# Row sums on VectorE in place of TensorE scores for the far cache rows of the sample attention

## The chip, the cores and the metric

The kernel runs on one core of a Trainium2 chip. The metric is the device time of one execution in microseconds (us). Engines are named as in the profile: PE is TensorE (with PEld, its weight loads), DVE is VectorE, ACT is ScalarE, POOL is GpSimd, SP is SyncE, which issues most DMAs here.

## The reference

One decoder layer is computed for a prompt of 2048 positions and for 8 sample batches of 8 new positions each. Each sample batch has its own cache of 2048 key rows and 2048 value rows of 8 heads by 64. The part that the change touches is the attention of the samples:

```python
DILATED_CONFIGS = ((128, 1), (512, 4), (2048, 16))
...
def _dilated_branch_sample(q, k_all, v_all, dil, n_strides):
    T = q.shape[1]
    E = q.shape[-1]
    w_buf = k_all.shape[1] - T
    idx = w_buf + jnp.arange(T)[:, None] - dil * jnp.arange(n_strides + 1)[None, :]
    valid = idx >= 0
    idx = jnp.maximum(idx, 0)
    kg = k_all[:, idx]
    vg = v_all[:, idx]
    s = jnp.einsum('bthe,btjhe->bthj', q, kg).astype(jnp.float32) * (E ** -0.5)
    s = jnp.where(valid[None, :, None, :], s, -jnp.inf)
    m = jnp.max(s, axis=-1, keepdims=True)
    p = jnp.exp(s - m)
    den = jnp.sum(p, axis=-1)
    o = jnp.einsum('bthj,btjhe->bthe', p, vg.astype(jnp.float32)) / den[..., None]
    lse = m[..., 0] + jnp.log(den)
    return o, lse
```

The three results are then mixed with weights proportional to their denominators. A cache row more than 512 positions back belongs to the configuration with distance 16 alone. New position t (0 to 7) reaches there the rows 16p + t and no others: such a row has exactly one query, and the rows 16p + 8 to 16p + 15 have none.

The rest is, for prompt and samples: RMS norm, one projection to 3584 columns (u, v, gate of mixer A; q, k, v, gate of mixer B), partial rotation of q and k, the spatial gate of mixer A, the three dilated attentions of the prompt, gates and norms, the product with w_out, the residual and a last norm.

## The kernel before

**Stages.** Up to about 95 us weights are loaded, scaled and split into two 16-bit parts (`load_weights`, whose VectorE steps are lines 202 to 220), and the tiles of x are scaled and split (`row_scale`, line 327, whose steps follow each other across POOL 334, DVE 335 and 336, PE 338 `ps_r`, DVE 340 `ss`, DVE 346 `dg`, PE 348 `ps_d`, ACT 350 `rb`). From there to about 390 us PE makes the q, k and v columns of 16 prompt tiles and one sample tile (products on line 265: 24 matmuls of 128x512 for a tile and a weight). From 390 to about 905 us runs the attention of the prompt and mixer A. From 905 us to the end come the gates, the merge of the three results and the products with w_out, again with line 265.

**The sample attention is filler.** `Sample` (line 469) is a generator. `Filler.pull` (line 94) is called for each product matmul and adds 216 times a rate to what is owed; each step of the generator pays `STEP1` = 250 (batches 0 to 4, beside the q, k, v products) or `STEP3` = 333 (batches 5 to 7, beside the last stage). So its instructions stand spread among the matmuls of line 265. What the generator hands out is then ordered by a scheduler on a simulated time line; every engine runs its list in order.

**One batch.** Cache keys come in five chunks of 2 rows by 128 partitions, 512 KB each (`load`, line 489, tile `kr`). Chunks g = 0 to 3 are the rows 16p + 2g and 16p + 2g + 1 for all 128 p, chunk 4 the other residues of the last 512 rows. For each chunk PE transposes the keys (line 594, eight 128x128 f32), ACT copies them out of PSUM (line 597, `kt`), PE multiplies them with `qbd`, the queries of two heads in a block-diagonal operand of 16 columns (line 498), and DVE adds the mask (line 506) into `sm`, which holds 11 slots of 64 scores for 128 partitions. `attend` (line 510) then takes the maximum (lines 515 to 521), subtracts it (527), exponentiates on ACT, sums (529, `ps_n` 534), and multiplies with the value rows (line 547: the values are the weights, 16 columns of `sm` move), whose result is scaled into `ott` (line 557). `vn` and `ktn` are the new positions' own values and keys. An f32 product of lines 498 and 547 is recorded as two matmuls, a transpose as one.

## Time and profile before

| | |
|---|---|
| median of three runs | 1214.53 us (1210.95 to 1216.84) |
| profiled execution | 1221.7 us, of which the span is 1219.6 us |
| mean granted TensorE clock | 0.965 of full speed |
| busy: PE, PEld | 1151.5 us (94%), 755.4 us (62%) |
| busy: DVE, ACT, POOL | 789.5 us (65%), 621.1 us (51%), 273.3 us (22%) |
| moved by DMA | 237.98 MB, mean 195 GB/s |

The span runs from the first to the last recorded instruction. Busy time of an engine is the sum over its instructions; overlapping matmuls are counted once. A share of the whole span is an average over stages that have different limits, so the rows further down are cut by stage.

### The profile page before, as it was taken

What the parts mean: (1) busy time and instruction counts of PE and PEld (TensorE: products, weight loads), DVE (VectorE), ACT (ScalarE), POOL (GpSimd) and SP (SyncE); (2) the same over time, 40 slices, a digit from 0 to 9 for tenths busy, and PEclk for the clock granted to TensorE, in tenths of its full rate; (3) what the DMA queues carried; (4) which work ended last, traced back from release to release, by engine and by line L of the source; (5) the groups of instructions that cost most, each with busy time, mean ns of one, the idle gap of its engine ahead of it and who ended that gap; (6) DMA issues with size and microseconds to landing.
All of it is one profiled execution on the core that took longest, in us unless ns stands there. A gap on an engine that the chain in (4) does not pass through costs nothing. (4 is left out here: it accounts for less than half of the span.)

```text
span 1219.6 us, 23145 instructions
## 1 busy us (share of the span) xinstructions
PE 1151.5 (94%) x8418; PEld 755.4 (62%) x8418; DVE 789.5 (65%) x2331; ACT 621.1 (51%) x1341; POOL 273.3 (22%) x294
## 2 busy tenths in 40 slices
PE   6689999999999998998999999799989999999997
PEld 2247777877767445665666676465636667676543
DVE  7853535444542677876887888867956565656773
ACT  5554434443442855765776767866754322322232
POOL 4422112112210032243334334432300000000110
PEclk9798999999997998998999999988999999999999
DMA  8667676767672997889979988987689868576652
GB/s 285 227 216 219 199 209 202 233 201 214 184 216 90 255 228 161 149 137 213 181 143 196 218 130 182 189 173 107 142 288 356 236 206 226 175 197 201 183 152 87
DMA packets 299026, 237.98 MB, mean 195 GB/s; under 512 B 189920, under 2 KB 240096, under 8 KB 298912
## 3 DMA queue, kind: packets, MB, share of 16 engines
q1 hardware_dynamic: 272848, 210.58, 68.8%
q10 hardware_dynamic: 26064, 25.92, 8.0%
q8 instruction: 66, 1.08, 0.4%
q14 instruction: 48, 0.39, 0.1%
HBM read 128.38 MB, written 63.24 MB: 157 GB/s over the span
## 5 line engine op out<-in xcount | busy, mean ns | idle before, releaser
L265 PEld LDWEIGHTS <-xh 128*128 128x128 f16 x2760 | 293.3, 113 | 222.8 <-issue 27.7
L934 DVE CUSTOM_DVE_ANT_0 sm<-ps_s,mk,qsi 128x256 f32<-128x256 f32 (+1 forms) x384 | 145.2, 420 | 64.1 <-PE ps_s L929 56.3
L942 ACT ACTIVATE sm<-sm,st 128x256 f32<-128x256 f32 (+1 forms) x384 | 145.7, 450 | 58.4 <-DVE st L937 53.2
L265 PE MATMUL ps_y<-wh_o,cT 128*128 128x512 f16 x528 | 169.0, 380 | 0.0
L964 POOL TENSOR_TENSOR p<-sm,p 128x256 f16<-128x256 f32 (+1 forms) x128 | 112.6, 886 | 233.0 <-ACT p L963 205.4
L498 PEld LDWEIGHTS ps_q<-qbd,kt 128*128 128x128 f32 x640 | 109.4, 191 | 22.9 <-issue 0.3
L153 POOL TENSOR_TENSOR sc<-sc,powers 128x1 f32<-128x1 f32 (+3 forms) x51 | 31.5, 618 | 410.0 <-DVE sc L1140 186.6
L547 PEld LDWEIGHTS ps_o<-sm,vr 128*128 128x128 f32 x640 | 108.2, 199 | 22.1 <-issue 1.3
L265 PEld LDWEIGHTS <-cT 128*128 128x128 f16 x800 | 82.0, 114 | 55.4
L265 PE MATMUL ps_y<-wl_o,cT 128*128 128x512 f16 x272 | 103.4, 380 | 0.0
L980 PE MATMUL ps_o<-vt,pT 128*128 128x65 f16 x600 | 79.5, 194 | 21.2 <-DMA pT<-p 21.2
L547 PE MATMUL ps_o<-sm,vr 128*128 128x16 f32 x640 | 92.6, 238 | 0.0
L498 PE MATMUL ps_q<-qbd,kt 128*128 128x16 f32 x640 | 91.9, 225 | 0.0
L265 PE MATMUL ps_p<-wh_k,xh 128*128 128x512 f16 x264 | 88.5, 386 | 1.6 <-ACT wh_k L217 1.5
L265 PE MATMUL ps_p<-wh_gb,xh 128*128 128x512 f16 x264 | 87.8, 388 | 1.2 <-DVE u L1069 1.0
L265 PE MATMUL ps_p<-wh_q,xh 128*128 128x512 f16 x240 | 83.8, 395 | 5.1 <-ACT xh L253 4.8
L265 PE MATMUL ps_p<-wh_v,xh 128*128 128x512 f16 x264 | 87.7, 378 | 0.3 <-DVE z L281 0.3
L265 PE MATMUL ps_p<-wh_va,xh 128*128 128x512 f16 x264 | 84.2, 385 | 1.9 <-ACT vt L383 1.3
L265 PE MATMUL ps_p<-wh_u,xh 128*128 128x512 f16 x264 | 83.9, 379 | 1.7 <-DVE z L281 1.7
L265 PE MATMUL ps_p<-wh_ga,xh 128*128 128x512 f16 x264 | 85.3, 385 | 0.0
L925 PE MATMUL ps_s<-k,q 128*128 128x256 f16 (+1 forms) x384 | 83.9, 258 | 0.4 <-DVE st L934 0.4
L929 PE MATMUL ps_s<-k,q 128*128 128x256 f16 (+1 forms) x384 | 82.8, 256 | 0.0
(308 smaller groups left out, 2544.1 us busy)
## 6 DMA issues: line engine op xcount, KB each, us to landing
vr<-cache_v SPq DMA_DIRECT2D x40, 512.0 KB
kr<-cache_k SPq DMA_DIRECT2D x40, 512.0 KB
xh<-xd SPq DMA_DIRECT2D x32, 512.0 KB
raw<-w_in SPq DMA_DIRECT2D x52, 256.0 KB
brd<-ob ACTq DMA_DIRECT2D x48, 264.0 KB
bt<-brd SPq DMA_DIRECT2D x16, 792.0 KB
vt<-vd ACTq DMA_DIRECT2D x48, 258.0 KB
vd<-vs SPq DMA_DIRECT2D x32, 258.0 KB
```

The costliest lines, as they stand in the source:

```text
L153: pool.tensor_tensor(out, src, powers[:out.shape[0], 0, 0:n], op=ALU.pow)
L265: ii = pe.matmul(out, l, r[:, k], start=(k == 0 and i == 0), stop=(k == 7 and i == len(ops) - 1))
L498: ii = pe.matmul(self.ps[:, c:c + 2 * T], k, ops[0][:, b, j], start=True, stop=True)
L547: ii = pe.matmul(po[:, j], v, sm[:, 2 * g + i, j * 2 * T:(j + 1) * 2 * T], start=False, stop=(g == NC - 1 and i == 2 and j == 3))
L925: ii = pe.matmul(out, q, kv[0], start=True, stop=False)
L929: keep(pe.matmul(out, q, kv[1], start=False, stop=True), "s")
L934: dve.tensor_tensor_reduce(sm[:, y].rearrange("p b k -> p (b k)")[:, 0:n], out, m, qsi[:, 3:4], -3e38, op0=ALU.add, op1=ALU.max, accum_out ...
L942: act.activation(sv, sv, AF.Exp, bias=self.st[:, 4 + u:5 + u], scale=1.0)
L964: (pool, dve)[x in DVELO].tensor_tensor(lo, sv, hi, op=ALU.subtract)
L980: keep(pe.matmul(po[:, u, 0:E + 1], hi, vv[:, vi, j, 0:E + 1], start=(b == 0), stop=False), "o")
```

## The change

The sample scores are split by the distance of the cache row. Rows below 1536 (`FAR` = 96 partitions of 16 rows, of which residues 0 to 7 are loaded) go to chunks g = 0 to 3; the last 512 rows, now as four rows to a partition, go to chunks 4 and 5. The order of the chunks in a batch is 0, 1, 4, 2, 3, 5.

- **Far chunk (32 in all).** Keys come as 96 partitions, 384 KB. A second DMA of 384 KB fills a tile `qb` with the two queries 2g and 2g + 1 of the batch, repeated on 96 partitions, read from a copy of the rotated queries in memory (`qsd`, a new DMA). DVE multiplies keys by queries in place (96x1024 elements) and reduces over the 64 elements of each head to 16 numbers a partition, straight into one slot of `sm`. There are no transposes, no copy, no score product and no mask. In `sm` the partitions 96 to 127 of that slot are set to a large negative number once a batch.
- **Near chunk (16 in all).** As before: eight transposes, two copies, eight score products (12 with the new rows in chunk 5), mask add.
- **Values.** All value products stay on PE. For a far row the weights are 96 rows high and only the two columns of `sm` that belong to the row's query and two heads move, instead of 16. The matmul count of a batch goes from 44 to 52 products, 32 of them of two columns.
- **Sizes.** `sm` has 6 slots in place of 11, so the maximum, subtract, exponential and sum run over 384 elements instead of 704. `dg` and `rb` of `row_scale` go from two buffers to one, `kt` in the last stage from four to three; there `qbd` holds three batches instead of eight.
- **Pace.** `STEP1` is 310, `STEP3` 480; a far chunk has four steps, a near chunk eight and its score steps. A batch has 116 steps in place of 139.

Over all eight batches the order lists of the two kernels hold: transposes 320 and 128, score products 352 and 160, value products 352 and 416 (256 of them far), copies on ACT 80 and 32, far multiplies and far reduces on DVE 0 and 32 each, cache loads 80 and 96 (the bytes are the same), `qb` loads 0 and 32.

The core of the diff:

```diff
-STEP1 = 250.0
-STEP3 = 333.0
-NK = 11
+STEP1 = 310.0
+STEP3 = 480.0
+NK = 6
+FAR = 96
...
-        dg = ph1.tile([P, P], F32, name="dg", tag="dg")
+        dg = ph1.tile([P, P], F32, name="dg", tag="dg", bufs=1)
...
-        rb = ph1.tile([P, P], F32, name="rb", tag="rb")
+        rb = ph1.tile([P, P], F32, name="rb", tag="rb", bufs=1)
...
+                if i == 0:
+                    sp.dma_start(qsd, qk)
...
-    NC = 5
+    NC = 6
+    FSTEP = 2
+    KORD = (0, 1, 4, 2, 3, 5)
...
         if g < 4:
-            return c[b].rearrange("(p r) c -> p (r c)", r=16)[:, 2 * g * W:(2 * g + 2) * W]
-        first = c[b, PAST - 4 * P + 8:PAST - 4 * P + 9, 0:1]
-        return bass.AP(tensor=c.tensor, offset=first.offset, ap=[[16 * W, 32], [2 * W, 4], [1, 2 * W]])
+            return c[b, 0:FAR * 16].rearrange("(p r) c -> p (r c)", r=16)[:, 2 * g * W:(2 * g + 2) * W]
+        return c[b, FAR * 16:].rearrange("(p r) c -> p (r c)", r=4)[:, 2 * (g - 4) * W:(2 * g - 6) * W]
...
+            if key == "kr" and g < 4:
+                q = self.qbs[u] = self.samk.tile([P, 2, W], F32, name="qb", tag="qb", bufs=2)
+                sp.dma_start(q[0:FAR].rearrange("p n c -> p (n c)"),
+                             qsd[b * T + 2 * g:b * T + 2 * g + 2].rearrange("t c -> (t c)")[None, :]
+                             .to_broadcast([FAR, 2 * W]))
...
+        def far(self, g, kr, qb, sm):
+
+            k = kr[0:FAR]
+            dve.tensor_tensor(k, k, qb[0:FAR], op=ALU.mult)
+            yield
+            o = sm[0:FAR, 0].rearrange("p (h t) -> p t h", t=T)[:, 2 * g:2 * g + 2]
+            dve.tensor_reduce(o, k.rearrange("p n (h e) -> p n h e", e=E), axis=AX.X, op=ALU.add)
+            yield
...
+                        c = slice(j * 2 * T, (j + 1) * 2 * T)
+                        if g < 4:
+                            t = slice(2 * g + i, None, T)
+                            ii = pe.matmul(po[:, j, t], vr[0:FAR, i, j * P:(j + 1) * P], sm[0:FAR, 0, c][:, t],
+                                           start=False, stop=False)
+                        else:
+                            v = (vr[:, i] if i < 2 else self.vn)[:, j * P:(j + 1) * P]
+                            ii = pe.matmul(po[:, j], v, sm[:, 2 * g - 7 + i, c],
+                                           start=False, stop=(g == NC - 1 and i == 2 and j == 3))
...
                     if g == 0:
                         sms[b] = self.sam.tile([P, NK, G], F32, name="sm", tag="sm", bufs=3)
+                        dve.memset(sms[b][FAR:, 0], NEG)
...
+                    if far:
+                        next(fw)
+                        for _ in range(FSTEP):
+                            yield self.step
+                    elif b is not None:
                         ps = psT.tile([P, 2, 2 * P], F32, name="ps_k", tag="T")
```

How the change moves instructions is shown at three places. Line numbers of the changed kernel are higher by 2 to 36 (265 is 267 there, 220 is 222, 212 is 214, 547 is 571 for far rows and 575 for near ones, 534 is 556).

**PE among the products of k**, in the stage from 95 to 370 us. `ps_p` is the product of x (`xh`) and a weight's high or low part (`wh_k`, `wl_k`), `ps_q` a score product. Before:

```order
L265 MATMUL ps_p<-wl_k,xh 128x512
L498 MATMUL ps_q<-qbd,kt 128x16
L265 LDWEIGHTS xh
L265 MATMUL ps_p<-wh_k,xh 128x512
L265 LDWEIGHTS xh
L265 MATMUL ps_p<-wh_k,xh 128x512
L498 MATMUL ps_q<-qbd,kt 128x16
```

After, among the products of the same weight:

```order
L267 MATMUL ps_p<-wl_k,xh 128x512
L571 MATMUL ps_o<-sm,vr 128x2
L267 LDWEIGHTS xh
L267 MATMUL ps_p<-wh_k,xh 128x512
L571 MATMUL ps_o<-sm,vr 128x2
```

Between two matmuls of line 265 there is still one instruction of the sample attention, but here a value product of two columns and not a score product of 16; the far chunks have none of the transposes and score products any more.

**DVE while the third weight (`wl_v`) is prepared**, between 51 and 68 us of the trace of before. `ws_v` and `wg_v` are its scales, `ropa` and `ropb` the rotation of q and k. Before:

```order
L210 TENSOR_SCALAR ws_v<-ws_v 128x1
L220 SCALAR_TENSOR_TENSOR wl_k<-raw,wg_k,wh_k 128x512
L211 RECIPROCAL ws_v<-ws_v 128x1
L213 TENSOR_SCALAR ws_v<-ws_v 128x1
L314 TENSOR_SCALAR qsi<-ws_v 128x1
L322 TENSOR_TENSOR ropa<-qk,ropc 128x128
L323 TENSOR_TENSOR ropb<-qk,rops 128x128
L212 TENSOR_SCALAR wg_v<-ng,ws_v 128x8
```

After:

```order
L529 TENSOR_REDUCE sm<-kr 96x2x8
L212 TENSOR_SCALAR ws_v<-ws_v 128x1
L342 TENSOR_SCALAR ss<-ps_r 128x1
L326 TENSOR_TENSOR qk<-ropa,ropb 128x8x8
L327 TENSOR_TENSOR qk<-ropa,ropb 128x8x8
L283 TENSOR_TENSOR z<-ps_p,z 64x512
L213 RECIPROCAL ws_v<-ws_v 128x1
L215 TENSOR_SCALAR ws_v<-ws_v 128x1
L316 TENSOR_SCALAR qsi<-ws_v 128x1
L526 TENSOR_TENSOR kr<-kr,qb 96x1024
L348 TENSOR_SCALAR dg<-ident,ss 128x128
L214 TENSOR_SCALAR wg_v<-ng,ws_v 128x8
```

The far multiply (line 526) and reduce (line 529) of the first chunks now stand in DVE's list between the steps of the scale `wg_v` (line 212 before, 214 after). In all, four far multiplies and three far reduces stand ahead of the last `wl_v` step.

**PE at the end of the q, k and v products**, where the last of batches 0 to 4 is finished; `ps_o` is a value product. Before:

```order
L265 LDWEIGHTS xh
L265 MATMUL ps_p<-wh_q,xh 128x512
L547 MATMUL ps_o<-sm,vr 128x16 x16
L547 MATMUL ps_o<-sm,vn 128x16 x4
L265 LDWEIGHTS xh
L265 MATMUL ps_p<-wh_q,xh 128x512
```

After:

```order
L267 LDWEIGHTS xh
L267 MATMUL ps_p<-wl_q,xh 128x512
L571 MATMUL ps_o<-sm,vr 128x2 x8
L267 LDWEIGHTS xh
L267 MATMUL ps_p<-wh_q,xh 128x512
L267 LDWEIGHTS xh
L267 MATMUL ps_p<-wh_q,xh 128x512
L575 MATMUL ps_o<-sm,vr 128x16
```

Ahead of these rows both lists have a run of 24 value products (16 columns wide before, two after). The second run, 20 products long before, is eight long after, with the remaining ones spread among the products that follow.

## Rows read from the trace of the kernel before

**Rows 1.** Stages: us; busy of PE, PEld, DVE, ACT, POOL; PEclk; DMA share; GB/s.

```profile
95.00:370.00 275.00, 275.00 (x1923) 209.55 (x1922) 124.78 (x271) 115.93 (x194) 48.66 (x45) 0.99 0.69 209
905.00:930.00 25.00, 22.80 (x127) 13.20 (x125) 19.51 (x46) 13.11 (x25) 1.40 (x2) 0.93 1.06 384
930.00:1206.00 276.00, 276.00 (x1658) 174.14 (x1657) 170.83 (x346) 82.88 (x182) 19.21 (x31) 0.99 0.69 199
```

**Rows 2.** PE's timeline: start us, us, engine, line, operation.

```profile
200.67 0.27 PE L594 MATMUL ps_k<-ident,kr 128*128 128x128 f32 x1
200.78 0.38 PE L265 MATMUL ps_p<-wh_v,xh 128*128 128x512 f16 x1
...
206.38 0.29 PE L498 MATMUL ps_q<-qbd,kt 128*128 128x16 f32 x2
206.52 0.38 PE L265 MATMUL ps_p<-wh_q,xh 128*128 128x512 f16 x1
...
207.11 0.28 PE L338 MATMUL ps_r<-ones,sq 128*128 128x1 f32 x2
207.25 0.59 PE L265 MATMUL ps_p<-wh_q,xh 128*128 128x512 f16 x2
```

**Rows 3.** PE's timeline where the q products end; columns as in group 2.

```profile
368.89 5.91 PE L547 MATMUL ps_o<-sm,vr 128*128 128x16 f32 x44
374.64 0.59 PE L265 MATMUL ps_p<-wh_q,xh 128*128 128x512 f16 x1
...
378.43 6.85 PE L547 MATMUL ps_o<-sm,vr 128*128 128x16 f32 x32
...
386.82 0.59 PE L265 MATMUL ps_p<-wh_q,xh 128*128 128x512 f16 x1
```

**Rows 4.** That stretch in steps of 5 us; columns as in group 1.

```profile
370.00:375.00 5.00, 5.00 (x37) 4.74 (x37) 0.00 (x0) 0.00 (x0) 0.00 (x0) 0.78 0.75 230
375.00:380.00 5.00, 5.00 (x18) 2.96 (x16) 1.61 (x5) 2.02 (x4) 0.00 (x0) 0.50 0.14 51
...
390.00:395.00 5.00, 5.00 (x26) 2.44 (x25) 1.50 (x9) 2.59 (x8) 0.00 (x0) 1.00 0.00 0
```

**Rows 5.** DVE by line: ns of one (least/median/most), first to last start.

```profile
L1293 DVE TENSOR_TENSOR bt<-bt x16: 672/682/694, 912.5 to 1181.2; 128x512 f32<-128x512 f32 x16
L1292 DVE TENSOR_TENSOR bt<-bt,f x16: 1749/1758/1760, 908.9 to 1178.9; 128x1536 f32<-128x1536 f32 x16
L515 DVE TENSOR_REDUCE mx<-sm x8: 1349/1362/1370, 127.8 to 1093.3; 128x64 f32<-128x704 f32 x8
L520 DVE TENSOR_REDUCE mx<-ps_x x8: 271/282/283, 134.6 to 1104.8; 64x1 f32<-64x128 f32 x8
L527 DVE TENSOR_TENSOR sm<-sm,ps_b x8: 880/887/889, 142.5 to 1109.4; 128x704 f32<-128x704 f32 x8
```

**Rows 6.** DVE's timeline while `wl_v` is prepared; columns as in group 2.

```profile
51.90 0.15 DVE L207 TENSOR_SCALAR ws_v<-ps_w 128x1 f32<-128x1 f32 x1
...
67.52 0.74 DVE L220 SCALAR_TENSOR_TENSOR wl_v<-raw,wg_v,wh_v 128x512 f16<-128x512 f32 x1
```

**Rows 7.** Two stretches around it; columns as in group 1.

```profile
65.00:70.00 5.00, 5.00 (x26) 2.30 (x25) 5.00 (x10) 2.81 (x5) 2.81 (x3) 1.00 0.69 195
...
70.00:95.00 25.00, 20.61 (x106) 11.52 (x105) 9.07 (x19) 11.85 (x22) 5.87 (x6) 0.96 0.73 224
```

**Rows 8.** What PE waited for, 85 to 370 us: total us, times, longest.

```profile
PE ps_d L348 <- DVE dg L346: 2.8, 1, 2.8
PE ps_k L594 <- ACT kt L597: 1.3, 1, 1.3
```

**Rows 9.** DVE, columns as in group 5; POOL's busy us, mean ns, idle before.

```profile
L336 DVE TENSOR_TENSOR sq<-sq x17: 221/292/1307, 8.0 to 325.3; 128x128 f32<-128x128 f32 x16, 128x64 f32<-128x64 f32 x1
...
L251 POOL TENSOR_TENSOR xt<-xt,rb 128x512 f32<-128x512 f32 x32 | 42.0, 1333 | 37.1 <-ACT rb L350 33.5 <-issue 3.6
```

**Rows 10.** SP's issues of the keys; columns as in group 5.

```profile
L489 SPq DMA_DIRECT2D kr<-cache_k x40: 328/399/4966, 46.0 to 1039.7; - x40
```

More of the change, by code (lines that the diff above doesn't have):

```diff
@@ L148, in kernel_body @@
     vsd = dram.tile([64, W], F32, name="vsd")
+    qsd = dram.tile([64, W], F32, name="qsd")
     hd = dram.tile([S + 64, W], F32, name="hd")
@@ L477, in __init__ @@
             self.sam, self.samk, self.step = sam, samk, step
-            self.mask = const(samk, "smask", [P, 10 + DB, T], a["c_smask"])
+            self.b0 = NB1 if sam is samk else 0
+            self.kts = 3 if sam is samk else 4
+            self.mask = const(samk, "smask", [P, 4 + DB, T], a["c_smask"])
             self.ps = pso.tile([P, W], F32, name="ps_q", bufs=1)
             self.po = pso.tile([P, 4, 2 * T], F32, name="ps_o", bufs=1)
-            self.raws = {"kr": {}, "vr": {}}
+            self.raws, self.qbs = {"kr": {}, "vr": {}}, {}
         def load(self, c, key, u):
@@ L488, in load @@
             r = self.raws[key][u] = pool_.tile([P, 2, W], F32, name=key, tag=key, bufs=3)
-            sp.dma_start(r.rearrange("p n c -> p (n c)"), cache_rows(c, *u))
+            b, g = u
+            n = FAR if g < 4 else P
+            sp.dma_start(r[0:n].rearrange("p n c -> p (n c)"), cache_rows(c, b, g))
+            if key == "kr" and g < 4:
[3 more added lines that the diff above has]
+                             .to_broadcast([FAR, 2 * W]))
         def scores(self, b, g, kts, sm):
-            o = (g // 2 % 2) * 4 + (g % 2) * 2
-            for i in range(2 if g < NC - 1 else 3):
+            x = g - 4
+            o = 4 * x
+            for i in range(2 + x):
                 for j in range(4):
@@ L537, in attend @@
             zero = ops[1][:, 0, DB * T:]
-            keep(pe.matmul(po.rearrange("p j c -> p (j c)"), self.raws["vr"][(b, 0)][:, 0, 0:P], zero,
+            keep(pe.matmul(po.rearrange("p j c -> p (j c)"), self.raws["vr"][(b, 0)][0:FAR, 0, 0:P], zero[0:FAR],
                            start=True, stop=False), "v")
@@ L545, in attend @@
                     for j in range(4):
-                        v = (vr[:, i] if i < 2 else self.vn)[:, j * P:(j + 1) * P]
-                        ii = pe.matmul(po[:, j], v, sm[:, 2 * g + i, j * 2 * T:(j + 1) * 2 * T],
-                                       start=False, stop=(g == NC - 1 and i == 2 and j == 3))
+                        c = slice(j * 2 * T, (j + 1) * 2 * T)
[7 more added lines that the diff above has]
+                                           start=False, stop=(g == NC - 1 and i == 2 and j == 3))
                         keep(ii, "v")
@@ L574, in batches @@
             bs = list(bs)
-            chunks = [(b, g) for b in bs for g in range(NC)]
+            chunks = [(b, g) for b in bs for g in KORD]
             nxt = iter(chunks)
@@ L587, in batches @@
                 kts = []
+                far = b is not None and g < 4
+                if far:
+                    fw = self.far(g, kr, self.qbs.pop((b, g)), sms[b])
                 for x in range(2):
-                    if b is not None:
+                    if far:
+                        next(fw)
+                        for _ in range(FSTEP):
+                            yield self.step
+                    elif b is not None:
                         ps = psT.tile([P, 2, 2 * P], F32, name="ps_k", tag="T")
@@ L595, in batches @@
                                 yield self.step
-                        kt = self.samk.tile([P, 2, 2 * P], F32, name="kt", tag="ktt", bufs=4)
+                        kt = self.samk.tile([P, 2, 2 * P], F32, name="kt", tag="ktt", bufs=self.kts)
                         act.activation(kt, ps, AF.Copy)
@@ L608, in batches @@
                         yield from self.stage(work)
-                if b is not None:
+                if b is not None and not far:
                     late.append((b, g, kts, sms[b]))
@@ L1388, in _constants @@
     t = np.arange(T)
-    p, i = np.arange(P), np.arange(10)[:, None]
-    key = np.where(i < 8, 16 * p + i, PAST - 4 * P + 16 * (p // 4) + 2 * (p % 4) + i).ravel()
+    p, i = np.arange(P), np.arange(4)[:, None]
+    key = (PAST - 4 * P + 4 * p + i).ravel()
     own = np.where(p // T == np.arange(DB)[:, None], PAST + p % T, 10 * PAST).ravel()
@@ L1394, in _constants @@
     n = sum(((dist >= 0) & (dist <= P * d) & (dist % d == 0)).astype(int) for d in (1, 4, 16))
-    m = np.where(n > 0, 8.0 * np.log(np.maximum(n, 1)), NEG).reshape(10 + DB, P, T).transpose(1, 0, 2)
+    m = np.where(n > 0, 8.0 * np.log(np.maximum(n, 1)), NEG).reshape(4 + DB, P, T).transpose(1, 0, 2)
     out["c_smask"] = np.ascontiguousarray(m.astype(f))
```

17 lines of the change are left out of this document (7 added, 10 removed).

## The prediction

> **What bounds the kernel now.** I read the busy time by stage first, since the averages over the span mix stages. From 95 to 370 us, where the q, k and v products run with five of the eight sample batches between them, PE is busy for 275.00 of 275.00 us, while DVE is busy for 124.78, POOL for 48.66, and the DMA share is 0.69 [rows 1]. From 930 to 1206 us, with the other three batches, PE is again busy throughout (276.00 of 276.00) and DVE for 170.83 [rows 1]. The waits of PE say the same: between 85 and 370 us there are two, 2.8 and 1.3 us [rows 8], and between 930 and 1206 us none. So in these two stages, half of the span, one us taken from PE's list is one us of time, as long as what takes its place elsewhere is not late. The sample attention is filler there: each of its PE instructions pushes the products of line 265 back by what it costs. The change has to be summed on PE, and DVE has to be tested for being late.
>
> **What an instruction costs PE.** Recorded durations overlap, so I read distances between starts, with a sample instruction between two products. A transpose moves the next product by 200.78 − 200.67 = 0.11 us, a score product (two records) by 206.52 − 206.38 = 0.14 us, and a two-record product of one column by 207.25 − 207.11 = 0.14 us [rows 2]. The last row matters: 1 column costs what 16 cost, so a two-column value product should cost 0.14 us too. Narrower value products are therefore no gain, and no loss either.
>
> **PE, the main sum.** Removed: 192 transposes × 0.11 = 21.1 us and 192 score products × 0.14 = 26.9 us. Added: 64 value products × 0.14 = 9.0 us. Net −39.0 us, of which five eighths (24) fall into the first stage and 15 into the last. If a removed score product had cost as much as a product in an unbroken run (below, 0.26 us) the gain would be larger; much of what is removed stands alone between two products, so I keep 0.14 and let this term run from −45 to −35.
>
> **The clock at the end of the q products.** There the last of the five batches is finished by two unbroken runs of value products: 22 of them from 368.89 to 374.64 (0.26 us each) and 20 from 378.43 to 386.82 (0.42 each) [rows 3]. The granted clock is 0.78 of full in 370 to 375, then 0.50, the 1.2 GHz level, and back at 1.00, the 2.4 GHz level, from 390 us [rows 4]. Nine products between the runs took 378.43 − 374.64 = 3.8 us, 0.42 each. Against 0.21 for a product and 0.14 to 0.2 for a value product, the stretch loses some 9 to 12 us. Changed, the first run is still there with 24 products, the second has eight, and the rest stands between products. Before, the clock rose within 3 us of mostly products after the second run; with the second run shortened, it should come back some 10 us sooner, or not if the spread value products keep it low. I take −4 us, from −8 to +2.
>
> **The start.** The scales of the third weight begin at 51.90 us, and its last low part is written from 67.52 to 68.26 us [rows 6]; products of that weight wait for it. DVE is full there, 5.00 of 5.00 us [rows 7]. The changed list puts four far multiplies and three far reduces ahead of that last low part, none of which has anything to hide under on DVE. Prices: a two-input operation on SBUF takes 682 ns for 512 elements and 1758 for 1536 [rows 5], 1.05 ns an element, so a multiply of 1024 takes 682 + 512 × 1.05 = 1.22 us. A reduce of 704 elements takes 1.362 us, 1.93 ns an element, and one of 128 takes 0.282 us [rows 5]; that gives 0.28 + 896 × 1.05 = 1.22 us as the low end (a step from one element to the next at the multiply's pace) and 1024 × 1.93 = 1.98 as the high end. The reduce of 704 reads with a stride and the far one reads contiguously, as the one of 128 does, so I take 1.3. Then 4 × 1.22 + 3 × 1.3 = 8.8 us come ahead of the third weight. PE is idle for 25 − 20.6 = 4.4 us in 70 to 95 us anyway [rows 7], part of which gives way to this delay: +5 us, from 0 to +12.
>
> **DVE in the two full stages.** 32 × (1.22 + 1.3) = 81 us are added. Per batch the maximum and the sum go from 1.36 to some 0.75 us, the subtract from 0.887 to some 0.5 [rows 5], and mask adds shrink, about 2 us, 16 in all. Net +65 us, 40 of it in the first stage. DVE then has 165 of some 250 us there, 66%, and 170.8 + 24 = 195 of 262 in the last stage, 74%. At the dearest prices (1.98 for the reduce, and 2.27 for a multiply that is 1.05 us longer) the 20 pairs of the first stage take 85 us: 125 + 85 − 10 = 200 of 250, still not the bound. DVE works in order, though, and behind each far multiply stand `ss` and `dg` of `row_scale`, the rotation, and the copies out of the products. A multiply whose keys or `qb` are late holds them all, and PE then waits at `ps_d` or at a product. The existing waits of that kind are 4.1 us together [rows 8]. I allow +1 us in the first and +2 us in the last stage, from 0 to +8.
>
> **What is taken at nothing.** Keys and values are the same bytes; 32 `qb` loads of 384 KB add 12.6 MB to 238. In the first stage 20 of them make 7.9 MB beside 209 GB/s × 275 us = 57 MB, which raises the share of 0.69 by some 0.1 [rows 1]. Only from 905 to 930 us are the engines of the DMA full (share 1.06, 384 GB/s [rows 1]); two to four loads fall there at about 1 us each: +2 us, 0 to +4. SP issues 49 more transfers at 0.40 us each [rows 10], 20 us in all; they lie beside PE's work as long as the loads come some chunks ahead of their use, and would cost those 20 us at most if each delayed a chunk that PE waits for. The 48 copies that ACT loses are off the path (115.93 of 275 us busy [rows 1]), and a single buffer for `dg` and `rb` costs nothing while a tile's `row_scale` is over before the next begins. The pace costs nothing either: 116 steps × 310 / (216 × 0.9) = 185 product matmuls a batch against 139 × 250 / 194.4 = 179 in the first stage, and with 480, 333 and a rate of 0.8 322 against 268 in the last, 967 in all of some 976 that there are; if the last batch came too late for them, its rest would run as an unbroken stretch, a few us.
>
> **Sum.** −39 − 4 + 5 + 1 + 2 + 2 = −33 us. For the profiled execution that is 1221.7 − 33 = 1189 us; it lies 7.2 us above the median of the three runs, 1214.53, against which the change will be timed, so 1214.5 − 33 = **1182 us**.
>
> **The rivals.**
>
> *DVE late on PE's path (slower).* If each far multiply stalls PE, by its transfers or by POOL, the gain goes at 33 / 32 = 1.0 us a multiply beyond what I have allowed. At 2 us each, 64 us, the time is 1214.5 − 33 + 64 = 1245. For it: `L336`, two inputs on DVE, takes 292 ns as a rule and 1307 at most, and the 32 POOL multiplications of line 251 are 1333 ns long [rows 9]; a far multiply is four times as long as most of DVE's steps there, and `row_scale` passes DVE, POOL and PE in turn. Against it: PE has 4.1 us of waits in the first stage now, with DVE idle for 275 − 125 = 150 us, and not one in the last stage, where DVE has 62% of the time filled. The Trainium skill ("SBUF — State Buffer", "Who interferes with whom") says that a DVE instruction with two SBUF inputs contends with a GpSimd instruction that reads SBUF. By that rule each of the far multiplies that meets line 251 is longer, and the spread of `L336` from 292 to 1307 ns agrees; but 20 × 1.0 us would leave DVE at 187 of 250 us, so it alone does not decide for this rival.
>
> *The two-column products are not cheap (no change).* If each of the 256 far value products costs the 0.26 us that one costs in an unbroken run [rows 3], since 24 to 32 of them come in a row with their own weights, 256 × 0.12 = 31 us come back: 1182 + 31 = 1213. For it: that run. Against it: the 0.14 us of a one-column product between products [rows 2], and that much of that run was slowed by the falling clock.
>
> *The start costs all of its delay and the clock does not come back earlier.* +12 and +2 in place of +5 and −4: 1182 + 13 = 1195. At the other end the delay is hidden, the clock is back early and PE's gain is 45: 1182 − 5 − 4 − 6 = 1167. Both are in the range.
>
> **How the numbers follow.** The forecast with its own spread, 1165 to 1203, gets 0.78, including both ends of the start; the no-change rival 0.08; DVE late 0.09, of which some third stays under its break-even; something unforeseen 0.05, on both sides. The forecast's own terms add up to −17 and +22 from 1182. The range 1165 to 1206 leaves about 0.2 out, mostly above. A measurement here tells from no change what is over 0.5%, 6 us: faster is below 1208.5. Faster 0.83, same 0.08, slower 0.09.
>
> **What would show it.** Right: no waits of PE in the two full stages, both shorter, by some 20 us and some 12; products 0.21 us apart with a two-column product at 0.14 between; far multiply and reduce near 1.2 and 1.3 us; DVE near two thirds busy in the first stage; the granted clock below 1.00 for less than 20 us at the end of the q products; first products of the third weight some 5 us later. Wrong: waits of PE for `dg`, for copies behind a far multiply or for a far reduce that sum to tens of us; two-column products 0.26 us apart; a stretch of sample work alone after the last product.

## The result and the profile after

The changed kernel takes 1224.6 us (median of 4 runs, 1220.99 to 1231.97) beside 1212.74 us of the kernel before on the same chip: a ratio of 1.0102, with a 95% interval from 1.0066 to 1.0138. It is **slower by 1.0%, some 12 us**, where 33 us less was forecast. Times and ratios, here and below, are of executions in the faster of the two states that this program shows. The profiled execution has a span of 1224.9 us at a mean granted clock of 0.954 (1219.6 us and 0.965 before).

The stages after, with the columns of [rows 1]:

```profile
95.00:370.00 275.00, 254.85 (x1581) 174.39 (x1579) 144.48 (x292) 92.05 (x148) 51.70 (x47) 0.95 0.76 218
905.00:930.00 25.00, 20.93 (x85) 8.99 (x84) 20.30 (x43) 10.21 (x19) 0.71 (x1) 0.86 1.06 278
930.00:1206.00 276.00, 269.63 (x1514) 159.97 (x1513) 185.69 (x366) 73.09 (x166) 19.33 (x31) 0.96 0.87 226
```

PE, which was busy in every microsecond of the two long stretches [rows 1], now idles for 20 us of the first and 6 us of the last, and its granted clock is 0.95 and 0.96 there, against 0.99. DVE is far from full (144 of 275 us in the first stretch). The DMA share rises to 0.76 and 0.87.

What PE waited for from 85 to 370 us, to set beside [rows 8] (total us, times, longest):

```profile
PE ps_d L350 <- DVE dg L348: 15.4, 5, 5.7
...
PE ps_p L267 <- ACT qk L373: 2.0, 1, 2.0
```

And what DVE waited for in the whole span, first line of the view:

```profile
DVE kr L526 <- DMA kr<-cache_k: 52.7, 20, 6.2
```

So PE waits for `dg`, and DVE, which makes `dg`, waits at 20 of the 32 far multiplies for their keys. The scene that repeats, on DVE's own timeline (start us, us; in brackets the idle time ahead and what ended it):

```profile
142.35 1.22 DVE L526 TENSOR_TENSOR kr<-kr,qb 96x1024 f32<-96x1024 f32 x1 [2.17 <-DMA kr<-cache_k]
143.50 0.28 DVE L348 TENSOR_SCALAR dg<-ident,ss 128x128 f32<-128x128 f32 x1
143.69 1.21 DVE L529 TENSOR_REDUCE sm<-kr 96x16 f32<-96x1024 f32 x1
...
152.25 1.22 DVE L526 TENSOR_TENSOR kr<-kr,qb 96x1024 f32<-96x1024 f32 x1 [4.42 <-DMA kr<-cache_k]
```

on SP's:

```profile
135.59 0.42 SPq L500 DMA_DIRECT2D kr<-cache_k  x1
...
144.93 0.33 SPq L500 DMA_DIRECT2D kr<-cache_k  x1
145.35 0.38 SPq L500 DMA_DIRECT2D vr<-cache_v  x1
153.50 0.31 SPq L503 DMA_DIRECT2D qb<-qsd  x1
154.11 0.35 SPq L231 DMA_DIRECT2D xt<-xT  x1
```

on PE's and on ACT's:

```profile
143.82 0.80 PE L350 MATMUL ps_d<-dg,ones 128*128 128x128 f32 x2 [1.59 <-DVE dg L348]
```

```profile
159.86 0.63 ACT L334 ACTIVATE sq<-xt 128x512 f32<-128x512 f32 x1 [9.88 <-DMA xt<-xT]
```

The load at 135.59 is used at 142.35, the next, at 144.93 (right after the reduce that began at 143.69 has ended), at 152.25: 7 us from issue to use, each time with DVE standing. `dg` at 143.50 stands behind the multiply and PE behind `dg`. After the load of values at 145.35 SP issues nothing until 153.50: the load of `qb` there needs the buffer that the multiply of 152.25 to 153.47 has just given back. A tile of x stands behind it, and ACT waits 9.88 us for it.

Where the time of the stages went (start of the first and of the last product, for two weights, before and then after):

```profile
L265 PE MATMUL ps_p<-wh_v,xh x264: 376/379/390, 66.9 to 413.0; 128*128 128x512 f16 x132
L265 PE MATMUL ps_p<-wh_q,xh x240: 376/378/634, 37.7 to 392.0; 128*128 128x512 f16 x120
```

```profile
L267 PE MATMUL ps_p<-wh_v,xh x264: 376/379/635, 66.9 to 419.2; 128*128 128x512 f16 x132
L267 PE MATMUL ps_p<-wh_q,xh x240: 375/379/635, 38.1 to 397.1; 128*128 128x512 f16 x120
```

The q products end 5 us later than before, where 24 us less of PE's work should have ended them earlier. By the same view it is 329 us against 325 from the first product of mixer B's gate to the last with w_out, and 4 us less than before between the two stages. These two executions are 5 us apart; the medians are 12 apart, so the stages tell where time went and not the whole of it.

### The profile page after: what moved, and what is told of

Its sections match the earlier page's. It is cut to its first block, busy times and chain, and to the rows that moved or that the text cites. A ratio compares the mean times of both kernels' runs of the same rounds, so it can differ in the third digit from the quotient of the medians.

```text
span 1224.9 us, 22319 instructions
## 1 busy us (share of the span) xinstructions
PE 1127.4 (92%) x7970; PEld 702.4 (57%) x7970; DVE 832.9 (68%) x2395; ACT 590.3 (48%) x1293; POOL 280.5 (23%) x294
## 4 chain that ended last, share of the span: by engine, by line
PE 56%; DMA 11%; DVE 7%; issue 4%; ACT 3%; POOL 1%; SPq 1%; POOLq 0%; ACTq 0%; DVEq 0%
PE ps_p L267 28%; PE ps_y L267 13%; DMA pT<-p 3%; DMA kr<-cache_k 2%; PE ps_o L571 2%; PE ps_s L961 2%; PE ps_s L965 2%; PE ps_t L990 2%; PE ps_o L575 1%; DMA xh<-xd 1%; PE ps_o L1016 1%; PE ps_o L1017 1%; DMA raw<-w_in 1%; PE ps_q L515 1%; PE ps_o L1018 1%
## 5 line engine op out<-in xcount | busy, mean ns | idle before, releaser
L267 PEld LDWEIGHTS <-xh 128*128 128x128 f16 x2760 | 284.0, 111 | 263.1 <-issue 50.7
L571 PEld LDWEIGHTS ps_o<-sm,vr 96*128 96x128 f32 x512 | 90.2, 201 | 24.0 <-issue 2.8
L1016 PE MATMUL ps_o<-vt,pT 128*128 128x65 f16 x600 | 78.7, 194 | 13.8 <-DMA pT<-p 13.8
L526 DVE TENSOR_TENSOR kr<-kr,qb 96x1024 f32<-96x1024 f32 x32 | 40.4, 1262 | 74.8 <-DMA kr<-cache_k 52.7
L961 PE MATMUL ps_s<-k,q 128*128 128x256 f16 (+1 forms) x384 | 82.2, 255 | 0.9 <-DVE st L970 0.9
L965 PE MATMUL ps_s<-k,q 128*128 128x256 f16 (+1 forms) x384 | 81.3, 253 | 0.0
L1017 PE MATMUL ps_o<-vt,pT 128*128 128x64 f16 x600 | 78.8, 195 | 0.0
L1018 PE MATMUL ps_o<-vt,pT 128*128 128x65 f16 x600 | 77.6, 193 | 0.0
```

The lines of the kernel that those rows point to most:

```text
L267: ii = pe.matmul(out, l, r[:, k], start=(k == 0 and i == 0), stop=(k == 7 and i == len(ops) - 1))
L526: dve.tensor_tensor(k, k, qb[0:FAR], op=ALU.mult)
L571: ii = pe.matmul(po[:, j, t], vr[0:FAR, i, j * P:(j + 1) * P], sm[0:FAR, 0, c][:, t], start=False, stop=False)
L961: ii = pe.matmul(out, q, kv[0], start=True, stop=False)
L965: keep(pe.matmul(out, q, kv[1], start=False, stop=True), "s")
L1016: keep(pe.matmul(po[:, u, 0:E + 1], hi, vv[:, vi, j, 0:E + 1], start=(b == 0), stop=False), "o")
```

## The experiments

Times are medians; the ratio is to the kernel before on the same chip, with its 95% interval. The kernel before had medians between 1212.7 and 1217.6 us in these measurements, so ratios are compared; 0.001 is 1.2 us. Diffs are against the changed kernel, shortened.

**Theory and rivals.** Late keys: DVE, in order, stands at far multiplies. Traffic: the transfers as such delay others. VectorE time: the 78 us of far work do. Start: the far work ahead of the third weight does.

### What is taken away

`nowait`: far work of the same size on a constant tile, no far keys, no repeated queries.

```diff
+            if key == "kr" and u[1] < 4:
+                self.raws[key][u] = None
+                return
...
-            dve.tensor_tensor(k, k, qb[0:FAR], op=ALU.mult)
+            k = self.scr[0:FAR]
+            dve.tensor_tensor(k, k, ones[0:FAR, None, :].to_broadcast([FAR, 8, P]), op=ALU.mult)
```

> The changed kernel with the far multiply and reduce of the same size on a constant tile; no far keys and no repeated queries are loaded, so the far scores of the reference are left out. Late-keys theory (VectorE, which works in order, stands at the far multiply until its keys land, and holds up the scale chain and the copies that TensorE needs): the waits go, time 1180 to 1195 us, waits of PE for dg and qk between 95 and 370 us under 6 us. VectorE-time theory (80 us more work on it is itself what delays): 1210 us or more. Start theory (the loss comes from the far work ahead of the third weight): 65 to 95 us stays as slow as in the changed kernel, time about 1205.

Measured: 1185.05 us, 0.9754 (0.9706 to 0.9802). Faster than the kernel before by nearly what was forecast. It loads less than either kernel, though: the 12.6 MB of far keys, which the kernel before loads too, are gone with the queries, so this is not PE's saving alone.

`loadsonly`: the same constant work, with all loads kept, into tiles that nobody reads.

```diff
-            k = kr[0:FAR]
-            dve.tensor_tensor(k, k, qb[0:FAR], op=ALU.mult)
+            k = self.scr[0:FAR]
+            dve.tensor_tensor(k, k, ones[0:FAR, None, :].to_broadcast([FAR, 8, P]), op=ALU.mult)
...
-                q = self.qbs[u] = self.samk.tile([P, 2, W], F32, name="qb", tag="qb", bufs=2)
+                q = self.qbs[u] = self.samk.tile([P, 2, W], F32, name="qb", tag="qb", bufs=1)
```

> The same constant far work, but all far keys and repeated queries are still loaded, into tiles that nobody reads; the far scores are left out. Late-keys theory: 1180 to 1200 us, within 10 us of the run without these loads. DMA-traffic theory (the 12.6 MB of repeated queries and the bursts slow other transfers and the products wait for those): 1210 to 1225 us.

Measured: 1216.94 us, 1.0038 (1.0007 to 1.0069). Against late keys as the only cause: nobody waits for these keys, and yet 32 us are gone, and the time lies in the range of the traffic theory.

`noqb`: keys loaded and waited for, no repeated queries.

```diff
-                q = self.qbs[u] = self.samk.tile([P, 2, W], F32, name="qb", tag="qb", bufs=2)
-                sp.dma_start(q[0:FAR].rearrange("p n c -> p (n c)"),
...
-            dve.tensor_tensor(k, k, qb[0:FAR], op=ALU.mult)
+            dve.tensor_tensor(k, k, ones[0:FAR, None, :].to_broadcast([FAR, 8, P]), op=ALU.mult)
```

> The changed kernel with the keys loaded and waited for, but multiplied by a constant instead of the repeated queries, which are not loaded; so the far scores are not those of the reference. Late-keys theory, buffers as cause (near chunks hold two of three key buffers until PE transposes them): 1210 to 1225 us, multiplies still wait for keys some 40 us in all. Late-keys theory, the load of the queries as cause (it stands ahead of the next keys in SP's queue, or takes their bandwidth): 1185 to 1200 us.

Measured: 1212.48 us, 0.9976 (0.9938 to 1.0013), and DVE waits 65.8 us for keys. The waits are not made by the load of the queries. Without it the kernel is all the same 0.0126, 15 us, faster than the changed one.

`nofar`: neither far work nor far loads; on top of the first lines of `nowait`:

```diff
-            dve.tensor_tensor(k, k, qb[0:FAR], op=ALU.mult)
...
-            dve.tensor_reduce(o, k.rearrange("p n (h e) -> p n h e", e=E), axis=AX.X, op=ALU.add)
...
-                        dve.memset(sms[b][FAR:, 0], NEG)
+                        dve.memset(sms[b][:, 0], 0.0)
```

> No far multiply, no far reduce, no far key and query loads; the far scores are a constant. Prices VectorE's own far work by the difference from the run with constant far work. Late-keys theory: within 8 us of that run, 1175 to 1190 us. VectorE-time theory: 20 us or more below that run. PE sum of the prediction (39 us of PE's work gone): about 1175 to 1180 us.

Measured: 1175.36 us, 0.9678 (0.9637 to 0.9718), 10 us below `nowait` (the intervals overlap). But `nowait` had lost more than that at the start: nothing held its far work back, and the first product of the third weight came at 79.1 us, against 66.9. The line of `nowait`:

```profile
L267 PE MATMUL ps_p<-wh_v,xh x264: 375/379/390, 79.1 to 388.7; 128*128 128x512 f16 x132
```

So VectorE's time as such is hardly the cause; a closer pair comes below. `keysonly` splits `loadsonly`: it is `nowait` without its first three lines, so that the far keys are loaded, unread, and no queries.

> Far work on a constant tile, no repeated queries, but the far keys are loaded, into tiles that nobody reads; the far scores are left out. Against noqb it takes away only VectorE's wait for the keys. Late-keys theory (VectorE stands at the far multiply for its keys): 1183 to 1195 us. Traffic theory (loads of the keys themselves, or SP's queue behind them, delay the tiles of x): 1205 to 1215 us.

Measured: 1206.38 us, 0.9938 (0.991 to 0.9967), in the range of the traffic theory, with the same 12 us lost at the start. `keysnofar` and `qbnofar` repeat the two without far work, and so without that loss: they are `nofar` with its loads put back, of the keys alone and of keys and queries.

> No far work on VectorE and no repeated queries, but the far keys are loaded into tiles that nobody reads; the far scores are left out. Against nofar (1175 us) it adds only 12.6 MB of key loads, the same bytes that the kernel before loads. If the loads compete with others once PE has less to do: 1188 to 1200 us. If they hide, and the 21 us between nowait and keysonly came of the far work that both put ahead of the third weight: 1175 to 1183 us.

Measured: 1189.83 us, 0.9812 (0.9771 to 0.9854): 16 us above `nofar`.

> As keysnofar, with the repeated queries loaded too, unread. Prices their 12.6 MB alone. If the two runs with and without queries that stand so far (loadsonly, keysonly) tell it right: 10 us above keysnofar. If VectorE's waits and not the traffic are the loss: within 4 us of it.

Measured: 1206.71 us, 0.9942 (0.9912 to 0.9973): 16 us more, where 10 or less than 4 were expected. Loads that nobody reads give their buffers back as they land, so that the next are issued at once; they crowd where the sample attention begins. The stretch from 65 to 95 us of `qbnofar`, columns as in [rows 1], has the DMA full and PE idle for 9 us:

```profile
65.00:95.00 30.00, 21.03 (x103) 10.46 (x101) 10.41 (x21) 10.79 (x19) 7.03 (x6) 0.85 1.01 302
```

Transfers cost time here, then; whether their bytes or their place in time do, these runs do not tell.

### Buffers, pace, place

`kr4`: a fourth key buffer in the first stage.

```diff
-            r = self.raws[key][u] = pool_.tile([P, 2, W], F32, name=key, tag=key, bufs=3)
+            r = self.raws[key][u] = pool_.tile([P, 2, W], F32, name=key, tag=key, bufs=3 if key == "vr" else 4 if self.b0 == 0 else 3)
...
-            self.kts = 3 if sam is samk else 4
+            self.kts = 3 if sam is samk else 2
```

> The changed kernel with four key buffers instead of three in the first stage, paid for with two instead of four buffers for copied near keys. Buffer theory: a far chunk's keys are loaded one chunk earlier there, waits of VectorE for keys in the first stage fall from 37 to under 15 us, 1205 to 1215 us with the last stage unchanged. Bunching or traffic theory: within 5 us of the changed kernel.

Measured: 1221.99 us, 1.0072 (1.0038 to 1.0106), not apart from the changed kernel. DVE's waits for keys up to 400 us are 36.4 us, against 36.7. The number of key buffers is not it, unless the two buffers of copied keys that it was paid with took back what it gave.

`pace7`: 14 steps for a far chunk instead of four.

```diff
-STEP1 = 310.0
-STEP3 = 480.0
+STEP1 = 231.0
+STEP3 = 357.0
...
-    FSTEP = 2
+    FSTEP = 7
```

> The changed kernel with 14 steps instead of 4 for a far chunk and the price of a step lowered so that a batch is handed out over as many products as before. Bunching theory (far chunks are consumed faster than the DMA brings them, so that loads crowd at the start of each stage): waits for keys under half of the changed kernel's 53 us, 1195 to 1210 us. Buffer theory (near chunks hold the key buffers until PE reaches them, whatever the pace): no change, 1218 to 1230 us.

Measured: 1217.54 us, 1.0047 (1.002 to 1.0075). Some 7 us better, at the edge of the two intervals, though DVE waits longer for keys (62.6 us): expected were half as long waits, a miss. `pace7kr4` joins both edits.

> Both edits together. If lateness of keys is the whole loss: 1190 to 1205 us, below the kernel before. If the load of the queries keeps the DMA full at the start of both stages: 1205 to 1220 us.

Measured: 1222.43 us, 1.0077 (1.0049 to 1.0105): no gain, and above both ranges.

The built order shows what neither touches. A far chunk needs no PE, so the scheduler puts its multiply as early in DVE's list as it takes the keys to be there, ahead of PE's place: three far chunks of the third batch come before PE's transposes of the last near chunk of the second. In the changed kernel's trace those multiplies start at 120.70, 131.95 and 142.35 us, the transposes at:

```profile
151.24 0.38 PE L630 MATMUL ps_k<-ident,kr 128*128 128x128 f32 x2
```

The two near chunks that wait for PE hold two of the three key buffers, and the far chunks take turns in the third: reduce, load, 7 us of landing, multiply. A fourth buffer would only let them run ahead by one more. `held2` therefore ties the multiply's place in the list to the products. It adds no wait on the chip.

```diff
-            dve.tensor_tensor(k, k, qb[0:FAR], op=ALU.mult)
+            ii = dve.tensor_tensor(k, k, qb[0:FAR], op=ALU.mult)
+            if tc_prod[0] is not None:
+                tc.add_manual_dep(ii.ins, tc_prod[0].name, AFTER, reason="not ahead of its place among the products")
```

> The changed kernel, with the scheduler told to place a far multiply not ahead of the product beside which it is handed out (no wait on the chip is added). Run-ahead theory (far chunks run ahead of the near ones, take turns in one key buffer, and each waits for keys that were issued 7 to 10 us before): near chunks give back their buffers in time, waits of VectorE for keys fall from 53 to under 20 us, 1195 to 1210 us. If lateness is a matter of traffic alone: within 6 us of the changed kernel.

Measured: 1209.02 us, 0.9961 (0.9932 to 0.9989). The waits for keys are nearly gone (one multiply waits 6.2 us more, for something that the profile puts down to a load of `xt`):

```profile
DVE kr L526 <- DMA kr<-cache_k: 5.4, 4, 2.8
```

`held7` is `held2` with the pace of `pace7`.

> As held2, with the even pace of pace7. If run-ahead and bunching are two causes: 1185 to 1200 us, faster than both kernels. If one cause: as held2 or pace7, whichever is lower. Traffic theory: 1210 to 1220 us.

Measured: 1196.61 us, **0.9856 (0.9817 to 0.9894)**: faster than both kernels, with the same instructions, bytes and buffers as the changed kernel. Place and pace gave back 0.0246, 30 us; place alone 17 us, the pace on top of it 13 us, and the pace without the place 7 us. The first stage of `held7`, columns as in [rows 1], and how long DVE waited for keys at the far multiplies in the whole span:

```profile
95.00:370.00 275.00, 263.12 (x1681) 181.49 (x1681) 152.83 (x310) 102.03 (x172) 57.60 (x46) 0.97 0.84 245
```

```profile
DVE kr L526 <- DMA kr<-cache_k: 4.4, 1, 4.4
```

The waits for keys are as short as in `held2`, so the 13 us of the pace did not come of them. Busy time in the pages of the changed kernel, `held2` and `held7`, whose spans are 1224.9, 1203.5 and 1190.3 us:

```profile
PE 1127.4 (92%) x7970; PEld 702.4 (57%) x7970; DVE 832.9 (68%) x2395; ACT 590.3 (48%) x1293; POOL 280.5 (23%) x294
PE 1128.1 (94%) x7970; PEld 703.8 (58%) x7970; DVE 838.3 (70%) x2395; ACT 591.9 (49%) x1293; POOL 277.6 (23%) x294
PE 1111.0 (93%) x7970; PEld 697.0 (59%) x7970; DVE 836.0 (70%) x2395; ACT 591.9 (50%) x1293; POOL 283.5 (24%) x294
```

The place takes 22 us off PE's idle time (97.5 to 75.4 us) and nothing off its busy time. The pace leaves PE as idle (79.3 us) and takes 17 us off the busy time of the same 7970 matmuls, at a mean granted clock of 0.966 against 0.953 in `held2`. So the place gave back waits, and the even pace gave back clock; the second is read from one profiled execution of each, and no run tested it by itself.

### What is left

Between `held7` and `nofar` 21 us remain. `held7nowait` and `held7noqb` are `held7` with the edits of `nowait` and `noqb`.

> held7 with the far work on a constant tile, and neither far keys nor repeated queries loaded; the far scores are left out. Prices VectorE's far work by the difference from nofar (1175 us), here without the 12 us that nowait lost at the start. VectorE's work free, as predicted: 1172 to 1180 us. VectorE's work costs: 1183 us or more. The difference from held7noqb is the price of the far keys' transfers.

Measured: 1171.03 us, 0.9638 (0.9573 to 0.9704), no more than `nofar`. VectorE's 78 us of far work cost nothing that shows where they stand in a good place; the two intervals leave some 9 us either way, and `nofar` has the old pace, so a small cost could hide behind the pace's gain. Both runs keep the single buffers of `dg` and `rb` and the three of `kt`, which are then not the loss either. PE is full again in the first stage:

```profile
95.00:370.00 275.00, 275.00 (x1790) 193.91 (x1788) 154.45 (x333) 113.07 (x193) 53.50 (x45) 0.98 0.66 193
```

> held7 without the repeated queries; the far keys are multiplied by a constant, so the far scores are not the reference's. If their 12.6 MB cost time as such: 8 to 17 us below held7 (1197 us), as between the earlier pairs with and without them. If with even placement the transfers hide, as the prediction took them at about nothing: within 4 us of held7.

Measured: 1181.08 us, 0.9712 (0.9653 to 0.9771). The keys' transfers are then some 9 us (0.0074; the two intervals overlap, so this one is not clear), the repeated queries 0.0144, 17 us. The other pairs with and without queries gave 12 to 16 us (0.0100 between `loadsonly` and `keysonly`, 0.0126 between the changed kernel and `noqb`, 0.0130 between `qbnofar` and `keysnofar`). Part of how they cost time is seen on ACT, whose first step on a tile of x waits for its load. From 95 to 370 us, in the kernel before, the changed one, `held7` and `held7noqb`:

```profile
ACT sq L332 <- DMA xt<-xT: 25.8, 10, 4.7
```

```profile
ACT sq L334 <- DMA xt<-xT: 59.2, 13, 10.6
```

```profile
ACT sq L334 <- DMA xt<-xT: 73.3, 14, 10.7
```

```profile
ACT sq L334 <- DMA xt<-xT: 36.4, 10, 7.6
```

With the queries a tile of x comes up to 10.7 us late and 73 us are waited for; without them it is 36. PE, which idles for 11.9 us of this stage in `held7`, idles for 1.1 us without them:

```profile
95.00:370.00 275.00, 273.86 (x1781) 192.51 (x1782) 156.39 (x332) 109.88 (x191) 54.39 (x46) 0.98 0.75 219
```

ACT's wait is not the price itself: in the pair `loadsonly` and `keysonly` it is 41.3 us with the queries and 53.8 without. Two more runs asked whether SP's queue does this, in which a load of queries waits for a buffer ahead of a tile of x. `held7qb3` has a third query buffer in the first stage, `held7kr4` a fourth key buffer.

```diff
-                q = self.qbs[u] = self.samk.tile([P, 2, W], F32, name="qb", tag="qb", bufs=2)
+                q = self.qbs[u] = self.samk.tile([P, 2, W], F32, name="qb", tag="qb", bufs=3 if self.b0 == 0 else 2)
```

> held7 with three instead of two buffers for the repeated queries in the first stage (two instead of four for copied near keys). If SP's queue, held by a load of queries that waits for its buffer, delays the tiles of x: ScalarE's wait for them falls from 73 to under 50 us between 95 and 370 us, 1185 to 1192 us. If the bytes are the price: within 4 us of held7 (1197 us).

Measured: 1193.18 us, 0.9841 (0.9796 to 0.9886); ACT's wait for x stays at 69.5 us.

> held7 with the same memory spent on a fourth key buffer. If SP's queue is held by loads of keys that wait for their buffer: 1185 to 1192 us. Otherwise within 4 us of held7 or a little above it for the smaller ring of copied keys.

Measured: 1190.26 us, 0.9822 (0.977 to 0.9874); 69.3 us. The time lies in the range given for a held queue, but neither run is apart from `held7`, and the wait does not fall. That a queue held by missing buffers is the price is not shown; the bytes, and the 32 more issues on SP, remain as explanations, and no run moved the loads to another queue or spread one load over several chunks.

## Why the prediction was wrong

The terms of the sum, each with the pair of kernels that prices it:

| term | predicted, us | measured, us | from |
|---|---|---|---|
| PE's work and the clock at the end of the q products | −39 − 4 | −44 | `held7nowait` and before |
| keys | 0 | +9 (not clear) | `held7noqb` and `held7nowait` |
| repeated queries | +2 | +17 | `held7` and `held7noqb` |
| pace of far chunks | 0 | +13 | `held2` and `held7` |
| VectorE's waits (place of far chunks) | +1 + 2 | +17 | changed and `held2` |
| the start | +5 | about 0 | changed and `held2` at 137 us |
| sum | −33 | +12 | |

The rows follow from one another like a chain from the kernel before to the changed one, so that their sum comes out right is no proof of its own. The first row holds more than PE: `held7nowait` also lacks the far keys' 12.6 MB, which the kernel before loads. With the second row it is −35, so PE and its clock gave 35 to 44 us. The ends of the prediction's own terms add up to −20 and +24 around its forecast, not to −17 and +22; neither reaches what was measured.

**PE was right.** A two-column value product among the products costs 0.14 us, as [rows 2] let expect of it, seen in the changed kernel's own timeline (330.18 − 330.04):

```profile
330.04 0.28 PE L571 MATMUL ps_o<-sm,vr 96*128 96x2 f32 x2
330.18 0.38 PE L267 MATMUL ps_p<-wh_v,xh 128*128 128x512 f16 x1
```

The no-change rival, that these products cost 0.26 us each, falls with it: 188 of the 256 stand alone between other instructions. In an unbroken run they do cost more, 5.09 / 22 = 0.23 us by the next line.

**The clock at the end of the q products came back early, as forecast**, to set beside [rows 3, 4]. Timeline and stretches of the changed kernel (the first run has 22 products in both traces, not 24):

```profile
381.37 5.09 PE L571 MATMUL ps_o<-sm,vr 96*128 96x2 f32 x44
```

```profile
380.00:385.00 5.00, 5.00 (x44) 4.63 (x41) 0.56 (x1) 0.00 (x0) 0.00 (x0) 1.00 0.72 203
385.00:390.00 5.00, 5.00 (x27) 3.54 (x27) 0.85 (x4) 0.77 (x2) 0.00 (x0) 0.66 0.84 257
390.00:395.00 5.00, 5.00 (x40) 4.10 (x40) 0.75 (x1) 0.64 (x1) 0.00 (x0) 1.00 0.18 70
```

In the kernel before, the two stretches that [rows 4] leaves out are:

```profile
380.00:385.00 5.00, 5.00 (x25) 5.00 (x25) 0.00 (x0) 0.00 (x0) 0.00 (x0) 0.50 0.14 52
385.00:390.00 5.00, 5.00 (x18) 2.99 (x18) 0.38 (x2) 0.00 (x0) 0.00 (x0) 0.51 0.00 0
```

One stretch of 5 us at 0.66 instead of 15 us at about half and 5 at 0.78. What this gave back in time was not measured by itself. But the clock now fell elsewhere, behind PE's new waits, which no term had: PE waits 5.67 us for `dg` up to 227.70, is busy for 4.33 of these 10 us, and the granted clock is 0.79 there and 0.87 in the next ten, part of the time at the lower of its two levels.

```profile
227.70 0.80 PE L350 MATMUL ps_d<-dg,ones 128*128 128x128 f32 x2 [5.67 <-DVE dg L348]
```

```profile
220.00:230.00 10.00, 4.33 (x20) 2.52 (x19) 5.94 (x14) 4.96 (x9) 2.89 (x3) 0.79 0.96 264
230.00:240.00 10.00, 10.00 (x64) 7.55 (x63) 2.70 (x6) 2.17 (x4) 1.44 (x2) 0.87 0.82 206
```

**VectorE's prices were right**: 1.22 us forecast and 1.221 measured for the multiply, 1.3 and 1.209 for the reduce.

```profile
L526 DVE TENSOR_TENSOR kr<-kr,qb x32: 1205/1221/1785, 54.5 to 1027.3; 96x1024 f32<-96x1024 f32 x32
L529 DVE TENSOR_REDUCE sm<-kr x32: 1201/1209/1219, 56.1 to 1031.0; 96x16 f32<-96x1024 f32 x32
```

The longest multiply is 0.56 us over the usual one. Three of the 32 took over 1.6 us, at 58.77, 89.43 and 111.10 us, and each overlaps a POOL operation that reads SBUF (line 336 or 253). That agrees with the rule of the Trainium skill that the prediction weighed ("SBUF — State Buffer", "Who interferes with whom", a VectorE instruction with two SBUF inputs against a GpSimd one that reads SBUF). Not each one that meets it is longer, as the prediction had it: those at 65.71 and 69.24 us overlap line 253 throughout and took 1.21. As forecast, it decides nothing.

**The first step that failed is VectorE's waits**: "I allow +1 us in the first and +2 us in the last stage, from 0 to +8". The text named the danger, a multiply whose keys are late with `ss` and `dg` behind it. `held2`, which takes the waits for keys from 52.7 to 5.4 us, gave back 17 us, 0.5 us a multiply. The rival *DVE late on PE's path*, whose break-even was 1.0 us a multiply, was given 0.09, for two reasons that do not bear on it. DVE's idle 150 us are no cover: an engine that works in order can be idle half the time and late at every multiply. And the 4.1 us of waits now [rows 8] belong to a kernel in which no DVE instruction waited for keys; they go to PE's transposes there, and none of PE's waits was for a load of keys. The evidence that was there to read is the built order: far multiplies of the third batch ahead of PE's transposes of the second, with three key buffers for both.

**The second is the pace**: "The pace costs nothing either". The prediction asked only whether the steps of a batch fit among the products, and not how evenly they come. Once the waits were gone, an even pace gave back 13 us more (`held2` and `held7`), by the pages as PE's granted clock.

**The third is the repeated queries**: "two to four loads fall there at about 1 us each: +2 us". The term counted full DMA engines only where the kernel before has them full, from 905 to 930 us. The first line of the queues in the two pages (packets, MB, share of 16 engines), before and after:

```profile
q1 hardware_dynamic: 272848, 210.58, 68.8%
```

```profile
q1 hardware_dynamic: 276768, 223.08, 75.6%
```

0.756 × 1224.9 − 0.688 × 1219.6 = 87 us more of all 16 engines' time, in stages whose x tiles come just in time: with share 0.84 in `held7`'s first stage they come up to 10.7 us late. A mean share below 1 was taken for cover. By which way these loads cost the 17 us stays open, as said above.

**The start** was read rightly, and yet cost next to nothing. The far work does stand ahead of the third weight: its last low part is finished at 74.67 us, 6.4 us later than before (68.26, [rows 6]).

```profile
73.93 0.74 DVE L222 SCALAR_TENSOR_TENSOR wl_v<-raw,wg_v,wh_v 128x512 f16<-128x512 f32 x1
```

Products of line 267 up to 95 us and from there to 137 us, in the changed kernel and in `held2`, whose first far multiply comes at 82.51 us (us; busy of PE, PEld; PEclk; DMA share; GB/s):

```profile
0.00:95.00 95.00, 42.24 (x150) 16.24 (x151) 0.86 0.87 264
95.00:137.00 42.00, 36.12 (x153) 15.45 (x151) 0.96 0.95 275
```

```profile
0.00:95.00 95.00, 49.14 (x194) 19.84 (x194) 0.89 0.83 249
95.00:137.00 42.00, 31.04 (x111) 12.71 (x112) 0.88 0.93 279
```

The changed kernel is 44 products behind at 95 us (and 27 behind the kernel before, which has 177), but at 137 us both have made about as many, 303 and 305. What it loses against `held2` it loses later. `nowait`, which has nothing to wait for and puts still more far work at the start, comes 12 us late to the third weight, the upper end that the prediction gave.

The net work added to DVE was 832.9 − 789.5 = 43 us, not 65. The lines of `sm` saved 16 us, as counted; the rest is in other lines, `dg` most of all (18.8 us before, 11.5 after), and was not looked into. That changes nothing.

## What to carry to other kernels

Work that is moved from the bounding engine to one with idle time brings its transfers to an engine that works in order: look at which load each moved instruction waits for, which buffer that load waits for, and who stands behind the instruction. Idle time and a mean DMA share below 1 are no cover for this. Where a scheduler places the moved work, keep it at its place among the work of the bounding engine and hand it out evenly; here that turned 1.0102 into 0.9856 with the same instructions. Look at the bounding engine's idle time and at its busy time by themselves: the first was given back by the place, the second by the pace.

## What was not expected of the hardware

A reduce of 1024 contiguous f32 elements to 16 sums takes 1.209 us, as long as a multiply of two inputs of that size (1.221); the 704 strided ones of [rows 5] took 1.362, 1.6 times as long for an element; whether the stride or the number of sums (64 against 16) makes it so is not shown. A value product of two columns from weights of 96 rows between two products costs PE the 0.14 us that a score product of 16 columns did. Repeated reads of the same bytes were no clear gain over reads of different ones. By the line of the first queue, `noqb` and `nowait` have:

```profile
q1 hardware_dynamic: 273184, 210.50, 71.6%
```

```profile
q1 hardware_dynamic: 269600, 197.91, 69.2%
```

The 32 loads of queries, 384 KB each, take 0.756 × 1224.9 − 0.716 × 1210.3 = 59 us of all 16 engines, 1.9 us each, and the 32 loads of far keys of the same size 0.716 × 1210.3 − 0.692 × 1176.5 = 52 us, 1.6 us each. The other three pairs, reckoned alike, give 42 to 58 us for the queries and 52 to 61 for the keys: the spread of the pairs is as large as the difference.
